# Decoder layer step on one core: the causal mask as a small matrix product, and the attention output stored in two halves

## The chip, the cores and the metric

The kernel runs on one core of a Trainium2 chip. A core has five engines with a queue of instructions each: PE (matrix products, with its weight loads listed as PEld), DVE (vector), ACT (scalar), POOL (GpSimd) and SP (which here issues most of the DMAs; POOL issues some). Each engine takes its queue in order and waits on semaphores of the others. PE writes its products into PSUM, in banks of 512 fp32 columns; DVE and ACT read PSUM, POOL does not. The metric is the device time of one execution in microseconds (us). Three runs of the kernel before gave 1462.22, 1463.86 and 1467.49 us, so the median is 1463.86 us.

## The reference, cut to what matters

```python
def fox_attend(q, k, v, cq, ck, q_pos):
    s = jnp.einsum('bqhd,bkhd->bhqk', q, k).astype(jnp.float32) * (HEAD_DIM ** -0.5)
    bias = jnp.transpose(cq, (0, 2, 1))[..., :, None] - jnp.transpose(ck, (0, 2, 1))[..., None, :]
    k_pos = jnp.arange(k.shape[1], dtype=jnp.int32)
    mask = k_pos[None, :] <= q_pos[:, None]
    s = jnp.where(mask, s + bias, NEG_INF)
    p = jax.nn.softmax(s, axis=-1).astype(v.dtype)
    return jnp.einsum('bhqk,bkhd->bqhd', p, v)
...
    q, k, v, logf, u = project_in(hp, w_in[i], b_f[i])
    att = fox_prompt(q, k, v, logf)                      # 8 heads, 1024 tokens, blocks of 128 rows
    ssm, sr, si = s5_mixer(u, h0, h0, *ssm_args)
    hp = post_mixer(hp, jnp.concatenate([att, ssm], axis=-1), p_prompt[i], *post_args)
...                                                      # the same for 32 sample tokens over a paged cache
    h1 = layer_norm(h + ..., ln1)                        # post_mixer: ALPHA*h + mix @ w_out, then the MLP
```

The model width is 1024: 512 columns of the mixer's output come from the attention over 8 heads of 64, and 512 from the state space part. Everything is fp32 to the outside.

## The kernel before, in words

fp32 precision is kept on PE by splitting an operand into a rounded part (type fp32r) and a rest: a product of two split operands is three products on PE (high by high, high by low, low by high). In the attention the scores are two products into one bank, of 68 and of 128 rows (line 872).

The program has these stages: layer norm and projections and the state space part (to about 310 us), the prompt's attention (about 310 to 516 us), the output projection with the second norm (to about 640 us), and the MLP (to the end). In the attention stage three streams are interleaved. `weights(h)` makes, for each of 8 blocks of 128 query rows, the scores of head h against all keys up to the diagonal: one bank when these are at most 512 keys, else two banks of equal width. The scores are held with the sign turned, so the softmax needs the row minimum `nm`, which is the bias of the exponential on ACT (line 882). A `tensor_reduce` on DVE takes the minimum over the first of two banks (line 876); over the last bank a `tensor_tensor_reduce` adds the mask tile `msk`, writes the masked scores back into the bank and takes the minimum at once (line 878; in the profile a CUSTOM_DVE instruction and a READ_ACCUMULATOR after it). The mask is 0 or +1e30, in the last 128 of 512 columns only. `values(h)` transposes the exponentials on PE (`tw`, line 900), copies them to SBUF on ACT (`pe`, line 904), rounds them on DVE (`ph`, line 905), takes the rest on POOL (`pl`), and multiplies both with the values, whose high and low parts lie side by side as 128 columns (lines 909, 910). So rows 0 to 63 of the bank `po` hold the high part's product and rows 64 to 127 the low part's. At the end of a half of 512 queries, ACT copies the low rows to `ol`, DVE adds them to the high rows into `oh`, and SP stores `oh` to `mixd` in DRAM (lines 912 to 916). There are 16 such halves. The third stream (`glu()` and `sample(bp)`) is background work that `fill` takes from by a time budget: the gate of the state space part, and the attention of the sample tokens, whose cache pages `pg` (64 of 256 KB) SP loads and whose value products are line 1035.

The output projection (`half`, line 1196) works through tiles of 128 tokens. For a tile it needs the state space columns of `mixd` (`load_mx`, line 1173), the attention columns (`load_at`, line 1213), which DVE multiplies by the reciprocal row sums `rb`, the split of both, and the split rows of `w_out` (`rawo`, `woh`, `wol`, from line 1157). Rows 512 to 1023 of `w_out` are loaded to a pool `woa`; rows 0 to 511 reuse memory of the attention's pool, so they come after the last half of the last head has been stored.

The order on each engine is not the order of the source: the build schedules the instructions of all engines by a model of their times, and memory that a tile takes over from another tile is part of what it waits for. A change of tile sizes or of operations therefore moves instructions elsewhere too.

Of the kernel before, what the change touches and what calls it, by code (L numbers as in the profile page):

```python
# [8 lines left out]
F32 = mybir.dt.float32  # L9
F32R = mybir.dt.float32r  # L10
# [4 lines left out]
AX = mybir.AxisListType  # L15
# [4 lines left out]
T = 1024  # L20
# [8 lines left out]
AW = 512  # L29
# [8 lines left out]
NEG = -1e30  # L38
# [3 lines left out]
IDENT, TRI, TRT, IOTA, SEL, QM, NM, BLK, OS, I16, OM, END = np.cumsum(  # L42
    [0, 128, 128, 128, 128, 256, 4, 4, 64, 16, 16, 512]).tolist()
# [26 lines left out]
def fox_s5_step(tc, a, o):  # L70
    nc = tc.nc
    V, S, G, PE, SY = nc.vector, nc.scalar, nc.gpsimd, nc.tensor, nc.sync
# [8 lines left out]
    def tt(e, out, x, y, op):  # L81
        e.tensor_tensor(out, x, y, op=op)  # L82
# [13 lines left out]
    MUL, ADD, SUB, MAX, MIN = ALU.mult, ALU.add, ALU.subtract, ALU.max, ALU.min  # L96

    cp = pool("const")
    dp = pool("dram", space=DRAM)
# [18 lines left out]
    cst = cp.tile([128, OM], F32, name="cst")  # L118
    ident = cst[:, IDENT:IDENT + 128]
# [3 lines left out]
    kkd = dp.tile([2, AW, NT], F32, name="kkd")  # L123
    vd = dp.tile([NT, AW], F32, name="vd")
    mixd = dp.tile([D, NT], F32, name="mixd")
    ud = dp.tile([4, 128, L * CB], F32, name="ud")
    yd = dp.tile([4, 128, L * CB], F32, name="yd")
    kd = dp.tile([NG, GH, 128], F32, name="kd")
# [81 lines left out]
    with ExitStack() as st0:  # L210
# [39 lines left out]
        for i, (t0, r) in enumerate(tiles):  # L250
# [3 lines left out]
            ps = bank2("pst").rearrange("p a (k c) -> p (a k) c", c=128)  # L254
# [11 lines left out]
            for k in range(KD):  # L266
                for j, (x, w) in enumerate(((hhi, wvh), (hhi, wvl), (hlo, wvh))):
                    if thin and j == 1:
                        PE.matmul(pv[:r], lhsT=x[:, k, t0:t0 + r], rhs=w[:, k], start=False, stop=(k == KD - 1),
                                  skip_group_check=True)  # L270
                    elif thin:
                        if j == 0:
                            PE.matmul(pv[:2 * r], lhsT=xx[:, k], rhs=w[:, k], start=(k == 0), stop=(k == KD - 1),
                                      skip_group_check=True)
                    else:
                        PE.matmul(pv[:r], lhsT=x[:, k, t0:t0 + r], rhs=w[:, k],
                                  start=(k == 0 and j == 0), stop=(k == KD - 1 and j == 2))
# [25 lines left out]
    with ExitStack() as st1:  # L303
# [20 lines left out]
        ps = flip()  # L324
# [114 lines left out]
        for dst, nm in ((crr, "c_re"), (cii, "c_im")):  # L439
# [3 lines left out]
            ps = flip()  # L443
# [6 lines left out]
        for dst, order in ((h0, ("state_re", "state_im")), (h0w, ("state_im", "state_re"))):  # L450
            t = ep.tile([128, 2, 2, HD], F32, tag="e", name="h0t")
            for j, nm in enumerate(order):
                SY.dma_start(out=t[:, :, j, :], in_=a[nm][0].rearrange("(u b) g p -> (b g) u p", u=2))
            ps = flip()
# [142 lines left out]
        def mixer(m):  # L597
# [65 lines left out]
            else:  # L663
# [7 lines left out]
                             in_=a["cache_logf"][0].rearrange("n t h -> n (t h)"),  # L671
# [27 lines left out]
        for c in range(3):  # L699
            ps = bank("mmf", "b")[0:40, :CH]  # L700
            for k in range(KD):
                for i, x in enumerate((hhi, hlo)):
                    PE.matmul(ps, lhsT=wf[:, k], rhs=x[:, k, c * CH:(c + 1) * CH],
                              start=(k == 0 and i == 0), stop=(k == KD - 1 and i == 1))
# [3 lines left out]
        ps = flip()  # L708
        for i, (t0, r) in enumerate(tiles):
# [16 lines left out]
                     in_=A[:, 0:64].rearrange("p (i h) -> p i h", h=8))  # L726
        SY.dma_start(out=a["o_fs"], in_=A[0:NS, 64:72])
        lf = ep.tile([8, NT], F32, tag="e", name="lf")
        for u in range(3):
            ps = flip()  # L730
            n = 4 if u < 2 else 1
            w_ = 0
            for i in range(n):
                t0, r = tiles[4 * u + i]
# [94 lines left out]
    aq_ = pool("attq", 2, stack=qctx, side="right")  # L829
# [2 lines left out]
    def slot(j, d=F32R):  # L832
        return (h1x, h1b)[j // 2].tile([128, 2 * L * CB], d, tag=f"u{j}", name="u", bufs=1)

    msk = aq_.tile([128, 512], F32, name="msk", bufs=1)
    G.memset(msk[:, 0:384], 0.0)
    G.tensor_copy(msk[:, 384:512], cst[:, TRI:TRI + 128])
    ins_, vs_, rows = {}, {}, {}

    def loads(h):  # L840
# [18 lines left out]
    def weights(h):  # L859
        qa, qb, ka, kb = ins_.pop(h)  # L860
        nm = ap_.tile([128, 8], F32, tag="nm", name="nm")
        for i in range(8):
            W = 128 * (i + 1)
            nb, n = (1, W) if W <= 512 else (2, W // 2)
            qs_ = slice(i * 128, i * 128 + 128)
            ss = []
            if nb == 2:
                nm1 = ap_.tile([128, 1], F32, tag="nm1", name="nm1")
            for c in range(nb):
                ps = bank("ss", "s")[:, 0:n]  # L870
                for x, y, kk in ((qb, kb, 68), (qa, ka, 128)):
                    PE.matmul(ps, lhsT=x[0:kk, qs_], rhs=y[0:kk, c * n:(c + 1) * n],
                              start=(kk == 68), stop=(kk == 128))
                ss.append(ps)
                if c < nb - 1:
                    V.tensor_reduce(out=nm1, in_=ps, axis=AX.X, op=MIN)
                else:
                    V.tensor_tensor_reduce(out=ps, in0=ps, in1=msk[:, 512 - n:512], scale=1.0,  # L878
                                           scalar=nm1 if c else -3.0 * NEG, op0=ADD, op1=MIN, accum_out=nm[:, i:i + 1])
            pr_ = ap_.tile([128, 512 * nb], F32, tag=f"row{nb}", name="row", bufs=4)  # L880
            for c, ps in enumerate(ss):
                S.activation(out=pr_[:, c * n:(c + 1) * n], in_=ps, func=AF.Exp, scale=-1.0, bias=nm[:, i:i + 1],  # L882
                             accum_out=lsum[:, h, i + 4 * c:i + 4 * c + 1])
            rows[h, i] = pr_
            yield

    def values(h):
        hs_ = slice(h * 64, h * 64 + 64)
        vr = vs_.pop(h)
        vv = ap_.tile([128, 8, 2, HD], F32R, tag="vv", name="vv")  # L890
        V.tensor_copy(vv[:, :, 0], vr)
        tt(G, vv[:, :, 1], vr, f(vv[:, :, 0]), SUB)
        for u in range(2):
            po = bank("po", "o")
            for j in range(4 * u + 4):
                i0 = max(j, 4 * u)
                n = 512 * (u + 1) - 128 * i0
                t = bank("tw", "t")[:, 0:n]
                for i in range(i0, 4 * u + 4):
                    PE.transpose(t[:, (i - i0) * 128:(i - i0) * 128 + 128], rows[h, i][:, j * 128:j * 128 + 128], ident)  # L900
                ph = ap_.tile([128, 512], F32R, tag="ph", name="ph", bufs=3)[:, 0:n]
                pl = ap_.tile([128, 512], F32R, tag="pl", name="pl", bufs=3)[:, 0:n]
                pe = ap_.tile([128, 512], F32, tag="pe", name="pe", bufs=4)[:, 0:n]
                S.copy(pe, t)
                V.tensor_copy(ph, pe)  # L905
                tt(G, pl, pe, f(ph), SUB)
                o = po[:, 512 - n:512]
                v = vv[:, j].rearrange("p a d -> p (a d)")
                PE.matmul(o, lhsT=v, rhs=ph, start=(j == 0), stop=False, skip_group_check=True)
                PE.matmul(o, lhsT=v, rhs=pl, start=False, stop=(j == 4 * u + 3), skip_group_check=True)  # L910
                yield
            ol = ap_.tile([64, 512], F32, tag="ol", name="ol", bufs=1)
            S.copy(ol, po[64:128])
            oh = ap_.tile([64, 512], F32, tag="oh", name="oh", bufs=2)
            tt(V, oh, po[0:64], ol, ADD)
            SY.dma_start(out=mixd[hs_, u * 512:u * 512 + 512], in_=oh)


    bg, bgt = [], [0.0, 0.0]
# [206 lines left out]
    ap_ = pool("att", 2, stack=actx)  # L1126
# [37 lines left out]
    for k in range(4, 8):  # L1164
        load_wo(k, woa, wp, V)
    mixv = mixd.rearrange("(k p) t -> p k t", p=128)
    dv = "p (c n) -> p c n"
    mxs, pss, order = {}, {}, [0, 1, 2, 3, 4, 5, 8, 6, 7]

# [40 lines left out]
    def load_at(i):  # L1210
        t0, r = tiles[i]
        mx = mxs[i][0]
        SY.dma_start(out=mx[:, 0:4, :r], in_=mixv[:, 0:4, t0:t0 + r])
        if t0 < T:
            rb = rbs.pop(i)
            tt(V, mx[:, 0:4, :r], mx[:, 0:4, :r], rb[:, :, :r], MUL)

# [3 lines left out]
    t = bank("trl", "t")[0:64, 0:128]  # L1221
# [12 lines left out]
    op = pool("out", 2, stack=smctx)  # L1234
# [47 lines left out]
    for n, i in enumerate(order):  # L1282
        t0, r = tiles[i]
# [20 lines left out]
        nb, rs = ln_norm(op, [z[:r, :512], z[:r, 512:]], r)  # L1304
# [20 lines left out]
    with ExitStack() as st1:  # L1325
# [24 lines left out]
        for m in range(8):  # L1350
# [21 lines left out]
            if m < 4:  # L1372
                k = m
# [369 lines left out]
```

## Time and profile before

| | |
|---|---|
| profiled execution | 1465.46 us |
| its span, first to last instruction | 1463.7 us |
| mean granted clock of PE | 0.979 of 2.4 GHz |
| PE busy | 1385.4 us (95%) |
| DVE busy | 993.2 us (68%) |
| ACT busy | 634.2 us (43%) |
| POOL busy | 675.1 us (46%) |

Busy time of PE is that of pipelined products, whose ends are modelled, so a product of 512 columns counts 0.4 us where the next one starts 0.23 us later. What a product costs in a dense stretch is read from the distance between the starts of neighbours, and lost time from the rows that name a wait. Idle time in brackets is that of the engine just before the instruction, with what ended it.

### The profile page before, as it was taken

Reading aid. Unit: us, or ns where it says so; the run is one execution under the profiler, and the core shown is the slowest. Engines: PE = TensorE matmul, PEld = TensorE weight load, DVE = VectorE, ACT = ScalarE, POOL = GpSimd, SP = SyncE. Lnnn points to the kernel's source line nnn. Section 1 sums busy time; section 2 is a strip of 40 time slices with the busy share of each in tenths; the row PEclk is TensorE's granted clock in tenths of the full one; section 3 lists DMA queues with packets and bytes.
Section 4 is the critical chain, followed back from the end, with each engine's and each line's share of the span. In section 5 each row is a group of like instructions: output and inputs, shape, how many; then the busy total and the mean of one; then the engine's idle time right before and its main releaser. Section 6 shows DMA issues by size and latency. Waiting matters only on the chain. (4 is left out here: it accounts for less than half of the span.)

```text
span 1463.7 us, 26623 instructions
## 1 busy us (share of the span) xinstructions
PE 1385.4 (95%) x10045; PEld 1269.7 (87%) x10045; DVE 993.2 (68%) x1591; ACT 634.2 (43%) x1188; POOL 675.1 (46%) x627
## 2 busy tenths in 40 slices
PE   6997999979999899999999999999999999999796
PEld 4787898977767657799999999999999999999786
DVE  8559599658867745568836545455455887878877
ACT  4423434446766624443324544444455344443212
POOL 4313012026665500037745443344337777777835
PEclk8999999999999999999999999999999999999998
DMA  7574355596776573222234344433376334444212
GB/s 278 174 139 103 97 146 140 165 245 174 180 190 156 150 245 91 80 74 87 79 99 154 133 147 162 162 124 134 134 277 212 119 126 153 162 162 133 74 32 101
DMA packets 205736, 211.89 MB, mean 145 GB/s; under 512 B 43592, under 2 KB 166088, under 8 KB 205608
## 3 DMA queue, kind: packets, MB, share of 16 engines
q1 hardware_dynamic: 197288, 178.02, 42.0%
q0 software_dynamic: 8320, 32.18, 5.7%
q8 instruction: 79, 1.29, 0.4%
q14 instruction: 49, 0.40, 0.1%
HBM read 143.59 MB, written 66.55 MB: 144 GB/s over the span
## 5 line engine op out<-in xcount | busy, mean ns | idle before, releaser
L1408 PE MATMUL pd<-x,a 128*128 128x264 f32 x1344 | 173.7, 289 | 14.2 <-DVE pacc L82 10.1
L1408 PEld LDWEIGHTS pd<-x,a 128*128 128x128 f32 x1344 | 169.5, 192 | 15.7 <-issue 10.0
L157 ACT CAST a<-s 128x256 fp32r<-128x256 f32 (+1 forms) x176 | 82.2, 483 | 200.5 <-POOL s L82 75.8
L82 DVE TENSOR_TENSOR pacc<-pd,pacc 128x528 f32<-128x528 f32 x180 | 121.4, 700 | 58.3 <-PE pd L1408 54.2
L82 DVE TENSOR_TENSOR wlo<-raw,whi 128x1024 fp32r<-128x1024 f32 x68 | 103.4, 1521 | 48.3 <-ACT whi L157 36.5
L1408 PE MATMUL pb<-th,a 128*128 128x264 f32 x768 | 132.3, 284 | 0.0
L82 POOL TENSOR_TENSOR pl<-pe,ph 128x512 fp32r<-128x512 f32 (+1 forms) x96 | 100.3, 1054 | 66.5 <-DVE ph L905 40.6
L82 POOL TENSOR_TENSOR a<-s,a 128x256 fp32r<-128x256 f32 x112 | 99.3, 892 | 60.4 <-ACT a L157 60.2
L82 POOL TENSOR_TENSOR s<-raw 128x256 f32<-128x256 f32 (+1 forms) x72 | 72.1, 1006 | 87.6 <-DVE a L82 64.0
L1408 PEld LDWEIGHTS pb<-th,a 128*128 128x128 f32 x768 | 109.2, 189 | 0.0
L1408 PE MATMUL pd<-x,whi 128*128 128x264 f32 x672 | 109.1, 284 | 0.0
L82 DVE TENSOR_TENSOR x<-x 128x1056 fp32r<-128x1056 f32 (+2 forms) x67 | 94.4, 1439 | 2.5 <-ACT x L1429 1.9
L183 PE MATMUL mmc<-hhi,whi 128*128 128x352 f32 x288 | 94.5, 328 | 0.0
L183 PE MATMUL mmc<-hhi,wlo 128*128 128x352 f32 x288 | 94.3, 327 | 0.0
L82 POOL TENSOR_TENSOR rs<-rs,mh 128x1 f32<-128x1 f32 (+1 forms) x27 | 20.5, 769 | 159.6 <-DVE rs L86 157.3
L1408 PEld LDWEIGHTS pd<-x,whi 128*128 128x128 f32 x672 | 93.7, 189 | 0.0
L183 PE MATMUL mmc<-hlo,whi 128*128 128x352 f32 x288 | 93.6, 325 | 0.0
L82 DVE TENSOR_TENSOR a<-s,a 128x512 fp32r<-128x512 f32 x64 | 48.0, 755 | 47.4 <-ACT a L157 43.2
L1408 PE MATMUL pb<-tl,a 128*128 128x264 f32 x384 | 78.1, 285 | 0.0
L157 ACT CAST whi<-raw 128x1024 fp32r<-128x1024 f32 x48 | 50.4, 1050 | 57.3 <-PE pa L1408 27.1
L882 ACT ACTIVATE row<-ss,nm 128x384 f32<-128x384 f32 (+4 forms) x96 | 55.5, 583 | 38.9 <-DVE nm L878 37.5
L1408 PE MATMUL pd<-x,wlo 128*128 128x264 f32 x336 | 68.2, 285 | 0.0
(471 smaller groups left out, 3959.9 us busy)
## 6 DMA issues: line engine op xcount, KB each, us to landing
x<-gd SPq DMA_DIRECT2D x53, 528.0 KB
raw<-in_w_up_dram SPq DMA_DIRECT2D x32, 512.0 KB
raw<-in_w_down_dram SPq DMA_DIRECT2D x128, 128.0 KB
gd<-e POOLq DMA_DIRECT2D x14, 1056.0 KB, 7.3
gd<-c POOLq DMA_DIRECT2D x14, 792.0 KB, 5.3
pg<-in_cache_k_dram SPq DMA_DIRECT2D x32, 256.0 KB
pg<-in_cache_v_dram SPq DMA_DIRECT2D x32, 256.0 KB
raw<-in_w_in_dram SPq DMA_DIRECT2D x12, 512.0 KB
```

The costliest lines, as they stand in the source:

```text
L82: e.tensor_tensor(out, x, y, op=op)
L157: S.copy(hi, x)
L183: PE.matmul(out, lhsT=wt[:, k], rhs=xt[:, k, c0:c0 + n], start=(k == 0 and i == 0), stop=(k == nk - 1 and i == 2))
L882: S.activation(out=pr_[:, c * n:(c + 1) * n], in_=ps, func=AF.Exp, scale=-1.0, bias=nm[:, i:i + 1], accum_out=lsum[:, h, i + 4 * c:i + 4 * ...
L1408: PE.matmul(ps[:, p, :PC], lhsT=wt[:, k], rhs=xt[:, k, p * PC:(p + 1) * PC], start=(start and k == 0 and j == 0), stop=(k == n - 1 and j = ...
```

## The change

Three things change in the source. The mask becomes a product on PE: an fp32r identity `idr_` as weights and a 128 by 128 fp32r mask tile `msk`, added into the last 128 columns of the last bank of each block; the row minimum is then a plain `tensor_reduce` per bank, and where there are two banks a `tensor_tensor` on 128 by 1 elements takes the smaller. The end of a half copies all 128 rows of `po` at once on ACT; SP stores the upper rows to `mixd` and the lower ones to a new DRAM tile `mixl`. The sum of the two is made in the projection: after the load of a tile's attention columns, POOL issues a DMA from `mixl` that adds into the loaded tile.

```diff
+    mixl = dp.tile([AW, T], F32, name="mixl")
...
-    msk = aq_.tile([128, 512], F32, name="msk", bufs=1)
-    G.memset(msk[:, 0:384], 0.0)
-    G.tensor_copy(msk[:, 384:512], cst[:, TRI:TRI + 128])
+    msk, idr_ = (aq_.tile([128, 128], F32R, name=n, bufs=1) for n in ("msk", "idr_"))
+    G.tensor_copy(msk, cst[:, TRI:TRI + 128])
+    G.tensor_copy(idr_, ident)
...
             if nb == 2:
-                nm1 = ap_.tile([128, 1], F32, tag="nm1", name="nm1")
+                nm1 = ap_.tile([128, 2], F32, tag="nm1", name="nm1")
             for c in range(nb):
                 ps = bank("ss", "s")[:, 0:n]
                 for x, y, kk in ((qb, kb, 68), (qa, ka, 128)):
                     PE.matmul(ps, lhsT=x[0:kk, qs_], rhs=y[0:kk, c * n:(c + 1) * n],
-                              start=(kk == 68), stop=(kk == 128))
+                              start=(kk == 68), stop=(kk == 128 and c < nb - 1), skip_group_check=True)
+                if c == nb - 1:
+                    PE.matmul(ps[:, n - 128:n], lhsT=idr_, rhs=msk, start=False, stop=True, skip_group_check=True)
                 ss.append(ps)
-                if c < nb - 1:
-                    V.tensor_reduce(out=nm1, in_=ps, axis=AX.X, op=MIN)
-                else:
-                    V.tensor_tensor_reduce(out=ps, in0=ps, in1=msk[:, 512 - n:512], scale=1.0,
-                                           scalar=nm1 if c else -3.0 * NEG, op0=ADD, op1=MIN, accum_out=nm[:, i:i + 1])
+                V.tensor_reduce(out=nm1[:, c:c + 1] if nb == 2 else nm[:, i:i + 1], in_=ps, axis=AX.X, op=MIN)
+            if nb == 2:
+                tt(V, nm[:, i:i + 1], nm1[:, 0:1], nm1[:, 1:2], MIN)
...
-            ol = ap_.tile([64, 512], F32, tag="ol", name="ol", bufs=1)
-            S.copy(ol, po[64:128])
-            oh = ap_.tile([64, 512], F32, tag="oh", name="oh", bufs=2)
-            tt(V, oh, po[0:64], ol, ADD)
-            SY.dma_start(out=mixd[hs_, u * 512:u * 512 + 512], in_=oh)
+            oh = ap_.tile([128, 512], F32, tag="oh", name="oh", bufs=2)
+            S.copy(oh, po)
+            SY.dma_start(out=mixd[hs_, u * 512:u * 512 + 512], in_=oh[0:64])
+            SY.dma_start(out=mixl[hs_, u * 512:u * 512 + 512], in_=oh[64:128])
...
+    mixlv = mixl.rearrange("(k p) t -> p k t", p=128)
...
         SY.dma_start(out=mx[:, 0:4, :r], in_=mixv[:, 0:4, t0:t0 + r])
         if t0 < T:
+            G.dma_start(out=mx[:, 0:4], in_=mixlv[:, :, t0:t0 + r], accum_op=ADD)
             rb = rbs.pop(i)
```

PE's queue at the start of head 0, blocks 0 to 2 (`ss` the score banks), before:

```order
L872 MATMUL ss<-kb,qb 128x128
L872 MATMUL ss<-ka,qa 128x128
L872 MATMUL ss<-kb,qb 128x256
L872 MATMUL ss<-ka,qa 128x256
L872 MATMUL ss<-kb,qb 128x384
L872 MATMUL ss<-ka,qa 128x384
```

The same place after the change, whose lines are numbered one higher from the new DRAM tile on:

```order
L873 MATMUL ss<-kb,qb 128x128
L873 MATMUL ss<-ka,qa 128x128
L876 MATMUL ss<-msk,idr__3106 128x128
L873 MATMUL ss<-kb,qb 128x256
L873 MATMUL ss<-ka,qa 128x256
L876 MATMUL ss<-msk,idr__3106 128x128
L873 MATMUL ss<-kb,qb 128x384
L873 MATMUL ss<-ka,qa 128x384
L876 MATMUL ss<-msk,idr__3106 128x128
```

One product of 128 columns is added behind the scores of each block, 64 in all.

POOL's queue at the end of the attention, with the last head's two halves of `pl` and the projection's norms (`rs`), before:

```order
L82 TENSOR_TENSOR pl<-pe,ph 128x512
L82 TENSOR_TENSOR pl<-pe,ph 128x384
L82 TENSOR_TENSOR pl<-pe,ph 128x256
L82 TENSOR_TENSOR pl<-pe,ph 128x128
L82 TENSOR_TENSOR pl<-pe,ph 128x512 x5
L82 TENSOR_TENSOR pl<-pe,ph 128x384
L82 TENSOR_TENSOR pl<-pe,ph 128x256
L82 TENSOR_TENSOR pl<-pe,ph 128x128
L82 TENSOR_TENSOR rs<-rs,mh 128x1 x6
```

The same place after the change (`mx<-mixl` are the adding loads):

```order
L82 TENSOR_TENSOR pl<-pe,ph 128x128
L1216 DMA mx<-mixl 128x4x128 x2
L82 TENSOR_TENSOR pl<-pe,ph 128x512 x5
L82 TENSOR_TENSOR pl<-pe,ph 128x384
L82 TENSOR_TENSOR pl<-pe,ph 128x256
L82 TENSOR_TENSOR pl<-pe,ph 128x128
L1216 DMA mx<-mixl 128x4x128 x2
L82 TENSOR_TENSOR rs<-rs,mh 128x1
L1216 DMA mx<-mixl 128x4x128
L82 TENSOR_TENSOR rs<-rs,mh 128x1
```

Two adding loads, of the projection's tiles 0 and 1, now stand in front of the `pl` of the last head's second half, and the other six stand among the norms.

PE's queue in the projection of the first tiles, where the last value products of the sample tokens (`po<-pg`) stand, before:

```order
L1035 MATMUL po<-pg,u 32x512 x2
L1196 MATMUL pso<-woh_6017,whi 128x512 x4
L1035 MATMUL po<-pg,u 32x512 x2
L1196 MATMUL pso<-wol_6018,whi 128x512
L1196 MATMUL pso<-woh_6017,wlo 128x512
L1196 MATMUL pso<-wol_6018,whi 128x512
L1196 MATMUL pso<-woh_6017,wlo 128x512
```

After the change they stand behind the last products with the state space rows of `w_out`, ahead of the first with the attention rows (`woh_6000`):

```order
L1197 MATMUL pso<-wol_5766,whi 128x512
L1197 MATMUL pso<-woh_5765,wlo 128x512
L1035 MATMUL po<-pg,u 32x512 x4
L1035 MATMUL po<-u,pnT 32x512 x4
L1045 MATMUL tpo<-cst,om 128x16 x4
L1197 MATMUL pso<-woh_6000,whi 128x512 x4
```

The scheduler has moved the second half of the sample attention ahead, so that its last products stand before the projection's attention rows instead of among and behind them. Four casts of `w_out` rows 512 to 1023, which stood at the end of the attention on ACT and DVE, stand early in the attention after the change.

## Rows read from the trace of the kernel before

**Rows 1.** Stretch table, attention: length, busy us (PE, PEld, DVE, ACT, POOL), clock, DMA.

```profile
310.00:520.00 210.00, 198.49 (x1336) 151.85 (x1336) 156.61 (x340) 129.11 (x345) 116.11 (x113) 0.96 0.70 175
```

**Rows 2.** Waits of PE's weight loads, 310 to 620 us: us in total, times, longest.

```profile
PEld po L1035 <- DMA pg<-in_cache_v_dram: 4.8, 3, 2.2
PEld po L910 <- POOL pl L82: 4.1, 6, 2.0
PEld pso L1196 <- ACT whi L1183: 3.9, 2, 3.1
PEld ss L872 <- ACT row L882: 3.7, 10, 0.8
...
PEld tw L900 <- ACT pe L904: 2.1, 4, 1.3
...
PEld po L909 <- DVE oh L82: 1.1, 1, 1.1
```

**Rows 3.** Timeline of PE around three products of 128 columns: start, us.

```profile
515.87 0.22 PE L910 MATMUL po<-pl,vv 128*128 128x128 f32 x1
515.93 0.45 PE L1196 MATMUL pso<-woh,whi 128*128 128x512 f32 x1
...
559.61 0.60 PE L1266 MATMUL psh<-cst,z 128*128 128x128 f32 x4
```

**Rows 4.** Groups of DVE in the attention stage: count, busy us, mean ns, idle before.

```profile
L878 DVE CUSTOM_DVE_ANT_0 ss<-ss,msk,nm 128x320 f32<-128x320 f32 (+3 forms) x32 | 20.9, 652 | 6.8 <-PE ss L872 5.5 <-ACT sg L1103 0.5 <-ACT pe L904 0.2
...
L876 DVE TENSOR_REDUCE nm<-ss 128x1 f32<-128x320 f32 (+3 forms) x32 | 18.6, 582 | 3.4 <-PE ss L872 3.4
...
L878 DVE CUSTOM_DVE_ANT_0 ss<-ss,msk 128x128 f32<-128x128 f32 (+3 forms) x32 | 15.8, 498 | 18.3 <-PE ss L872 11.7 <-PE po L910 4.3 <-ACT sg L1103 1.5
...
L82 DVE TENSOR_TENSOR oh<-po,ol 64x512 f32<-64x512 f32 x16 | 10.8, 676 | 3.5 <-ACT ol L913 3.5
...
L878 DVE DVE_READ_ACCUMULATOR2_ANT nm<- 128x1 f32 x64 | 8.8, 137 | 0.0
```

**Rows 5.** Timeline of DVE: an operation on 128 by 1 elements.

```profile
551.37 0.16 DVE L91 SCALAR_TENSOR_TENSOR nb<-mv,rs 128x1 f32<-128x1 f32 x1 [0.37 <-POOL rs L82]
```

**Rows 6.** Groups of ACT by shape, attention stage: copies from PSUM.

```profile
L904 ACT COPY pe<-tw 128x512 f32<-128x512 f32 x48 | 26.9, 592 | 7.5 <-PE tw L900 6.3 <-POOL pl L82 1.1
...
L913 ACT COPY ol<-po 64x512 f32<-64x512 f32 x16 | 9.3, 583 | 4.6 <-PE po L910 4.3
```

**Rows 7.** Timeline of PE in the projection, 530 to 542 us.

```profile
530.46 1.09 PE L1196 MATMUL pso<-woh,whi 128*128 128x512 f32 x4
...
535.20 1.04 PE L1035 MATMUL po<-pg,u 128*32 128x512 f32 x2 [1.79 <-DMA pg<-in_cache_v_dram]
537.12 1.73 PE L1035 MATMUL po<-pg,u 128*32 128x512 f32 x2 [0.87 <-DMA pg<-in_cache_v_dram]
538.77 2.07 PE L1196 MATMUL pso<-woh,whi 128*128 128x512 f32 x4
540.77 1.05 PE L1035 MATMUL po<-pg,u 128*32 128x512 f32 x4
```

**Rows 8.** Timeline of ACT at the end of the attention.

```profile
516.13 0.58 ACT L913 COPY ol<-po 64x512 f32<-64x512 f32 x1 [2.66 <-PE po L910]
...
521.89 1.05 ACT L157 CAST woh<-rawo 128x1024 fp32r<-128x1024 f32 x1 [1.03 <-DMA rawo<-in_w_out_dram]
```

**Rows 9.** Timeline of SP's DMAs at the end of the attention: start, us to issue.

```profile
517.46 0.49 SPq L916 DMA_DIRECT2D mixd<-oh  x1
518.04 1.50 SPq L1160 DMA_DIRECT2D rawo<-in_w_out_dram  x3
```

**Rows 10.** Operations of POOL, ns min/median/max: the subtraction `pl`, and a DMA it issues.

```profile
L82 POOL TENSOR_TENSOR pl<-pe,ph x96: 447/1164/3095, 328.6 to 509.4; 128x512 fp32r<-128x512 f32 x48, 128x384 fp32r<-128x384 f32 x16, 128x256 fp32r<-128x256 f32 x16, 128x128 fp32r<-128x128 f32 x16
...
L1515 POOL DMA_DIRECT2D gd<-e x14: 781/781/788, 784.6 to 1046.6; - x14
```

**Rows 11.** DMA issues of POOL in the program: size, us from issue to landing.

```profile
accd<-sgp POOLq DMA_DIRECT2D x8, 528.0 KB, 3.0
```

## Prediction

> **What bounds the kernel now.** I read the stretch table first, to see which engine is full where the change acts. In the attention PE is busy 198.49 of 210 us, DVE 156.61, ACT 129.11, POOL 116.11, at 0.96 of the upper clock level, 2.4 GHz [rows 1]. So an instruction added on PE costs its own time, and one taken from another engine gives only what PE waited for it. That is read from the second view, the waits of PE's weight loads [rows 2]: pages of the cache 4.8 us, `pl` 4.1, the state space split `whi` 3.9, `row` 3.7, `pe` 2.1, `oh` 1.1. These waits, not the 56 us of DVE work that disappears, are all that the change can win. The timelines of PE and ACT then show how the attention hands over to the projection.
>
> The profiled execution took 1465.46 us; the sum is made against it. It lies 1.6 above the median of the runs, 1463.86, to which I apply the result.
>
> **1. The mask on PE.** 8 heads by 8 blocks are 64 products of 128 columns. A single one starts 0.06 us before its successor, 515.87 to 515.93 [rows 3]; four that follow each other take 0.60 us where one takes 0.22, so (0.60 − 0.22) / 3 = 0.13 us each with nothing between [rows 3]. The products of masks stand between wide ones, like the first row, but their weights must be loaded too. I take 0.085, nearer the single one: 64 × 0.085 = **+5.4 us**, with ends 64 × 0.06 = +3.8 and 64 × 0.13 = +8.3. All of it is on PE and nothing covers it but the waits of step 2.
>
> The Trainium skill, page "TensorE: Matmul & The Clock Gate", section "Back-to-back issue gap", puts the spacing in a stream of weight load and product pairs at about 81 ns for 128 columns. As an estimate of that page the term would be 64 × 0.081 = 5.2 us; the trace's two rows lie on either side of it.
>
> **2. DVE.** Gone are the two forms of the fused minimum, 20.9 + 15.8 us, their 64 register reads, 8.8, and 16 sums `oh`, 10.8: 56.3 us [rows 4]. New are 32 reductions on the second of two banks, of the shape of the present first ones, 32 × 0.582 = 18.6 [rows 4]; 32 on a single bank, for which I take the fused one less the difference seen between the forms, 0.498 − (0.652 − 0.582) = 0.428, so 13.7; and 32 minima on 128 by 1 at 0.16, 5.1 [rows 4, 5]. That makes 37.4, net −18.9 of 156.6 us. DVE isn't the bound, so the 18.9 counts only through PE's waits for the chain from scores over `row` and `pe` to `pl`: 3.7 + 2.1 + 4.1 + 1.1 = 11.0 us [rows 2]. The first product after the scores sees its minimum earlier by 0.137 + 0.07 us less 0.16, next to nothing for two banks, and by 0.2 for one; the bank of `po` no longer waits for ACT and then DVE (0.583 + 0.676), but for one copy of 0.592 [rows 4, 6]. What is late next are the pairs of `pl` on POOL, which the change leaves alone. I take about half, **−5 us**, between 0 and −11.
>
> ACT copies 128 rows where it copied 64: 592 against 583 ns [rows 6], nothing. SP issues 16 more stores of 0.49 us [rows 9], 7.8 us of a queue that has 210; hidden, while the pages do not stand behind a store that waits for ACT.
>
> **3. The sample attention moved ahead.** Today its last value products stand among the projection's first. There PE waits for pages (4.8 us in three waits [rows 2], two of them seen as idle time of PE, 1.79 and 0.87 [rows 7]), and after the waits a run of products goes at about half speed: 2.07 for four `pso` where 1.09 is normal and 1.73 for two page products where 1.04 is, 1.7 us in all [rows 7]. In the new order most page products stand in the last head, and the last four behind all products with the state space rows. So 4.8 + 1.7 = 6.5 can go; against that the pages must now land earlier, while the attention already uses the DMA engines at 0.70 of their time [rows 1], and a page that is late there is a wait of the same kind. I take **−6 us**, between 0 and −6.5.
>
> **4. The state space columns.** PE waits 3.9 us, once for 3.1, for `whi` [rows 2], the split of the first tiles. In the new order these products begin in the last half but one, and the four casts of `w_out` which stood on ACT at the end are early. I take **−3 us**, between 0 and −3.9. It is not more because ACT, freed there, takes the copies of 128 rows next.
>
> **5. The end of the attention.** The last half is copied (0.58 [rows 8]), stored twice (2 × 0.49 [rows 9]), and only then may the rows 0 to 511 of `w_out` and the tiles 4 to 7 be loaded. From the issue of `rawo` at 518.04 to its cast at 521.89 are 3.85 us [rows 8, 9], and the cast takes 1.05. That is 0.58 + 0.98 + 3.85 + 1.05 = 6.5 us. PE has behind its last `po` 12 products at (1.09 − 0.45) / 3 = 0.21 us [rows 3, 7] and eight page and closing products, together some 4.5 us; so 2 us are uncovered, where today pages filled them. The subtraction for `wol` may add one more.
>
> The added wait is on POOL: two adding loads stand ahead of the last eight `pl`, and behind them waits PE's `po`. POOL is held from the copy of the half before: 0.58, stores 0.98, their landing 3.0 (as an estimate that of a DMA to DRAM that POOL issues [rows 11]), SP's load 0.49 and landing 3.0, two issues at 0.78 [rows 10], and the first `pl`, 1.16: 10.8 us. PE has in that time 25 projection products (5.3), 25 transposes (at 0.11 to 0.13, about 3), six page products (some 3): 11.3. It is just covered. The other six loads stand among single-column norms and delay nothing that is urgent. Together **+3 us**, between 0 and +8, where +8 is an uncovered 6.5 and 1.5 of the hold.
>
> Sum: 5.4 − 5 − 6 − 3 + 3 = −5.6, so 1459.9 for the profiled execution and **1458 us** for the median. Best ends: 3.8 − 11 − 6.5 − 3.9 = −17.6; worst: 8.3 + 8 = +16.3.
>
> **The rivals.**
> *The masks eat the gain (about 1464).* PE's waits may only change their name: DVE freed of 12% gives −2 instead of −5, and the pages moved into the attention wait there for half of the 6.5. Then 5.4 − 2 − 3 − 3 + 3 = +0.4. For it speaks that PE has 198.49 busy of 210 us [rows 1]; against it that `whi` and two page waits are single gaps at one place which the new order leaves.
>
> *POOL's adding loads decide (about 1472, slower).* POOL's `pl` takes 1164 ns in the median but up to 3095 [rows 10]: something holds POOL. If an issue is stretched the same way, from 0.78 to 3.1, the two in front of `pl` add 4.6 to a hold of 10.8 and PE waits 4.1; of the six others the four of the second half come when nothing is loaded ahead and add 4 × 2.3 = 9.3 behind the attention. −5.6 + 4.1 + 9.3 = +7.8. It decides from the point where the hold passes the 11.3 us of cover. Against it: the 14 issues of `gd` lie between 781 and 788 ns [rows 10], none stretched, though in a stretch where DVE does other work.
>
> The Trainium skill, page "SBUF — State Buffer", section "SBUF: two separate sides", says that a DMA issued by GpSimd is starved of its descriptors while DVE holds the port that the two share. By that rule this rival would hold, and the attention, where DVE is busy three quarters of the time, is the place. The issue rows at hand don't show it, the spread of `pl` agrees.
>
> *More goes than I count (about 1449).* If the chain had slack only where DVE was late, all 11.0 go: 5.4 − 11 − 6.5 − 3.9 + 1 = −15. For it: the waits for `row`, ten of them, are short, below 0.8 us [rows 2], the size of one DVE instruction. Against it: the longest for `pl` is 2.0 and belongs to POOL.
>
> *The change doesn't act as written:* the scheduler's new order could wait for something that the order doesn't show. I count it with the first rival.
>
> **How the numbers follow.** About 0.5%, 7.3 us, is what a measurement of this kernel can tell from no change. Forecast 0.47 (own range 1453 to 1463; 0.20 of it faster by over 0.5%, 0.26 within, 0.01 slower), masks eat the gain 0.18 (0.01, 0.15, 0.02), POOL's loads 0.17 (0.02 within, 0.15 slower), more goes 0.18 (all faster). Sums: faster 0.39, within 0.43, slower 0.18. The range reaches from beyond the third rival, 1447, to near the second, 1470.
>
> **What would show it.** Step 1: 64 products of 128 columns, whose successors start 0.06 to 0.13 us after them. Step 2: DVE busy near 138 us in the attention, and less in the waits for `row`, `pe` and `pl`. Step 3: no wait for pages among the projection's products; if the waits for pages in the last two heads rise by as much, it failed. Step 4: no wait for `whi` over 1 us. Step 5: between the last `po` and the first product with the attention's rows of `w_out` a gap of 2 to 3 us, and no wait of PE for POOL at the last half's first `pl`; the adding loads' issue at 0.78 us. The forecast is wrong if PE waits there for several us, or if the attention stage as a whole gets longer than 210 us.

## The result and the profile after: slower by 20 us

The changed kernel takes 1486.16 us in the median of 4 runs (1484.23 to 1491.36), the kernel before 1465.67 in the same comparison. The ratio is 1.0137 with a 95% interval of 1.0111 to 1.0163, so +20 us over before, where 1458 was forecast, and beyond the upper end of the range, 1470. The profiled execution has a span of 1489.6 us against 1463.7, that is +25.9.

The place is quickly found. The products of the projection with all 128 rows begin later and end later. Each line gives count, duration in ns (least, median, most), first and last start in us, and the form; first the changed kernel, then the kernel before:

```profile
L1197 PE MATMUL pso<-woh,whi x128: 391/396/796, 515.7 to 653.7; 128*128 128x512 f32 x128
```

```profile
L1196 PE MATMUL pso<-woh,whi x128: 389/396/792, 507.8 to 630.1; 128*128 128x512 f32 x128
```

23.6 of the 25.9 us are lost by there. The stretch tables of the changed kernel, the first stretch to be held against [rows 1]:

```profile
310.00:520.00 210.00, 196.26 (x1323) 152.61 (x1324) 140.62 (x280) 120.55 (x332) 110.41 (x105) 0.95 0.67 171
```

```profile
520.00:660.00 140.00, 130.46 (x609) 96.09 (x608) 71.42 (x145) 52.36 (x103) 25.49 (x25) 0.95 0.55 140
```

and the second stretch of the kernel before:

```profile
520.00:660.00 140.00, 136.23 (x713) 104.49 (x712) 76.45 (x156) 57.44 (x113) 17.75 (x18) 0.99 0.40 119
```

DVE fell from 156.61 to 140.62 us, near the 138 foreseen, but PE, ACT and POOL did less as well: in the same 210 us less of the work got done. PE's clock fell from 0.99 to 0.95 behind 520. The waits of PE's weight loads, 310 to 620 us (total, times, longest), against [rows 2]:

```profile
PEld po L911 <- POOL pl L82: 7.4, 12, 1.3
PEld po L1035 <- DMA pg<-in_cache_v_dram: 6.7, 2, 5.4
...
PEld ss L873 <- ACT row L883: 5.3, 8, 1.8
...
PEld ssm L973 <- DVE u L86: 4.1, 1, 4.1
...
PEld pso L1197 <- ACT whi L1184: 0.7, 1, 0.7
```

The waits for `pl`, for pages and for `row` all grew (4.1, 4.8 and 3.7 before), where the forecast let them shrink; a single wait for the first vector of the sample tokens (`u`) takes 4.1 us, where 0.7 was. The wait for `whi` shrank, from 3.9 to 0.7. What DVE does for the minima, as groups of its instructions from 310 to 556 us (busy us, mean ns):

```profile
L878 DVE TENSOR_REDUCE nm<-ss 128x1 f32<-128x384 f32 (+4 forms) x96 | 51.9, 552 | 29.8 <-PE ss L876 23.3 <-PE ss L873 5.5
L82 DVE TENSOR_TENSOR nm<-nm 128x1 f32<-128x1 f32 x32 | 12.4, 387 | 0.2
```

The reductions cost 51.9 us, as foreseen (18.6 kept, 18.6 and 13.7 new, together 50.9). But the 32 minima on 128 by 1 elements take 387 ns each and not the 160 of [rows 5]. One of them, with what stands around it, from the timeline of all engines (start, us):

```profile
409.74 0.63 DVE L878 TENSOR_REDUCE nm<-ss 128x1 f32<-128x448 f32 x1
...
410.53 0.97 DVE L906 CAST ph<-pe 128x384 fp32r<-128x384 f32 x1 [0.17 <-PE ss L873]
...
411.43 0.68 DVE L878 TENSOR_REDUCE nm<-ss 128x1 f32<-128x512 f32 x1
411.65 0.99 POOL L82 TENSOR_TENSOR pl<-pe,ph 128x384 fp32r<-128x384 f32 x1 [0.36 <-DVE ph L906]
...
412.03 0.63 DVE L82 TENSOR_TENSOR nm<-nm 128x1 f32<-128x1 f32 x1
...
412.69 0.63 ACT L883 ACTIVATE row<-ss,nm 128x448 f32<-128x448 f32 x1 [0.64 <-DVE nm L82]
```

Two things are to be seen. The second bank's minimum is there at 410.37, but the instruction that combines both stands behind a cast and behind the next block's reduction, and starts at 412.03. And then it ends with POOL's `pl`, at 412.66. The exponential, which frees the score banks, waited 2.3 us for an operation of 0.15. Of the 32 minima in this trace 15 begin while POOL is idle (one of them 0.02 us before the end of a `pl`) and take 150 ns on average. The other 17 begin beside a running operation of POOL, end within 0.03 us of the end of that or the next one, and take 595.

The Trainium skill, page "SBUF — State Buffer", section "SBUF: two separate sides", says that a DVE operation with two inputs in SBUF and a GpSimd operation that reads SBUF share a port pair as an exclusive lock, and that whichever starts second is blocked for the whole of the other. The rows agree: 0.15 us alone, and to the end of `pl` beside it.

### The profile page after: what moved, and what is told of

The parts are those of the page before. It is cut to its first block, busy times and chain, and to the rows that moved or that the text cites. A ratio compares the mean times of both kernels' runs of the same rounds, so it can differ in the third digit from the quotient of the medians.

```text
span 1489.6 us, 26703 instructions
## 1 busy us (share of the span) xinstructions
PE 1400.1 (94%) x10109; PEld 1283.0 (86%) x10109; DVE 986.2 (66%) x1543; ACT 632.5 (42%) x1188; POOL 689.2 (46%) x635
## 5 line engine op out<-in xcount | busy, mean ns | idle before, releaser
L82 POOL TENSOR_TENSOR pl<-pe,ph 128x512 fp32r<-128x512 f32 (+1 forms) x96 | 103.5, 1087 | 82.8 <-DVE ph L906 63.8
L82 POOL TENSOR_TENSOR s<-raw 128x256 f32<-128x256 f32 (+1 forms) x72 | 75.4, 1051 | 85.2 <-DVE a L82 63.8
L906 DVE CAST ph<-pe 128x512 fp32r<-128x512 f32 (+1 forms) x96 | 52.4, 561 | 31.7 <-ACT pe L905 20.1
```

## Experiments

Theories at the start: Q, the waits in SP's queue and for pages; M, the 64 products; H, the halves with POOL's adding loads. From the second group of kernels on: L, the minimum's wait for POOL; O, chance of the scheduler's order; C, the separate minimum lets other work in between. Differences in us are the ratio times 1466.

**mask_only.** The mask part of the change with the old end of a half.

```diff
-            S.copy(oh, po)
...
+            S.copy(ol, po[64:128])
...
+            tt(V, oh, po[0:64], ol, ADD)
...
-            G.dma_start(out=mx[:, 0:4], in_=mixlv[:, :, t0:t0 + r], accum_op=ADD)
```

> Only the mask product and the plain minimum; the halves are summed on DVE and stored once, as before. Theory Q (queues and waits: of the +20 us the 64 products are about 5, the rest is waiting that the new order makes, at SP's stores and pages): +5 to +12 us over before. Theory M (the 64 products on a full PE are most of the loss): +15 to +20. Theory H (two stores per half and POOL's adding loads are most of it): +5 or less.

1486.14 us, ratio 1.0137 (1.0102 to 1.0172): the whole loss, +20. H falls, Q's range is passed, and M's upper end is met.

**halves_only.** The other part alone: `S.copy(oh, po)`, two stores and the adding load, with the mask as before.

> Only the copy of both halves, the two stores and the adding loads; the mask as before on DVE. Q: +5 to +12 us over before, with waits of PE for pages or for what stands behind a store on SP. M: 0 or a gain of some us. H: +13 or more, with PE waiting for the pl behind POOL's adding loads.

1470.68 us, ratio 1.0026 (1.0009 to 1.0042): +4, with an interval of 1.3 to 6.2, so at the low end of what Q wanted or under it, and far from H's +13.

**no_mask_product.** The changed kernel without the products.

```diff
-                if c == nb - 1:
-                    PE.matmul(ps[:, n - 128:n], lhsT=idr_, rhs=msk, start=False, stop=True, skip_group_check=True)
```

> The changed kernel without the 64 mask products, so the scores are not masked; the reductions and all else stay. Q: 5 us less than the changed kernel (about 1481), give or take what a shifted order does. M: 15 us less or more (1471 or below). H: 5 less.

1490.47 us, ratio 1.0163 (1.0129 to 1.0197). The scores are then not masked, so it serves for timing alone. It is no faster without the products (the interval overlaps that of the changed kernel), where all three theories wanted less time: M falls. What is left for the loss is what DVE got, or the order.

**act_stores.** Both stores of a half on ACT: `S.dma_start` for `SY.dma_start`.

> The changed kernel with both stores of a half issued by ACT, which made the copy, instead of SP, so that SP's loads of heads and pages no longer stand behind a store that waits for ACT. Q: 5 to 10 us less than the changed kernel (1476 to 1481), and the 3.7 us wait for the sample's first vector near 353 us gone. M and H: no change beyond 0.3%, or a little slower for 32 more issues on ACT.

1489.44 us, ratio 1.016 (1.0126 to 1.0194). Against Q: taking the stores out of SP's queue gained nothing. The wait for the sample's first vector was gone, but PE stood 3.4 us before the same product, now for `row`.

**one_bank_only** and **two_bank_only.** Mask product and plain minima only in blocks with one bank, or only in blocks with two. Only the latter have the 128 by 1 minimum.

```diff
+                if nb == 1:                                 # in two_bank_only: if c == 1
+                    PE.matmul(ps[:, n - 128:n], lhsT=idr_, rhs=mskr, start=False, stop=True, skip_group_check=True)
```

> The kernel before with the mask product and plain minimum only in the 32 blocks of one bank; blocks of two banks stay as before, so no 128x1 minimum exists. L: 0 to +4 us over before (32 products, 2.5 us). O: +8 or more is possible, as another order.

> The kernel before with the mask product, plain minima and 128x1 minimum only in the 32 blocks of two banks. L: most of the loss, +14 to +20 us over before. O: not more than the kernel with the one-bank blocks changed.

1466.68 us, ratio 1.0001 (0.9988 to 1.0013), and 1484.49 us, ratio 1.0122 (1.0095 to 1.0149). The loss lies in the two-bank blocks, as L wanted.

**before_plus_min** and **before_plus_reduce.** The kernel before with 32 more instructions that change no value, once with two operands, once with one (there the fused minimum writes to the second column of `nm1`, which is two columns wide):

```diff
+            if nb == 2:
+                tt(V, nm[:, i:i + 1], nm[:, i:i + 1], nm1, MIN)                       # before_plus_min
+                V.tensor_reduce(out=nm[:, i:i + 1], in_=nm1, axis=AX.X, op=MIN)       # before_plus_reduce
```

> The kernel before with one more 128x1 minimum of nm and nm1 behind each masked reduction over two banks (32 in all, the value does not change). L: +8 us or more over before. O: another order by chance, so anything from 0 to +10, not tied to the durations of these 32.

> The kernel before with 32 more reductions over a 128x2 tile at the places of the 32 extra minima of the run before (before_plus_min, +21 us). Every engine has the same instructions in the same order as there; only the kind of these 32 differs (one operand in SBUF instead of two). Theory L (the wait of the two-operand form for POOL makes the loss): +0 to +5 us over before. Theory O (the order makes it): +16 or more, as there.

1487.91 us, ratio 1.0139 (1.012 to 1.0157), and 1482.62 us, ratio 1.009 (1.007 to 1.011). The first run shows the loss without any product or any change of the reductions over the scores. In the two traces the instructions stand in the same order on every engine, and the two intervals do not meet, so their 7 us are the two operands' alone. The groups of DVE, first with two operands, then with one:

```profile
L82 DVE TENSOR_TENSOR nm<-nm,nm 128x1 f32<-128x1 f32 x32 | 12.2, 381 | 0.2
```

```profile
L882 DVE TENSOR_REDUCE nm<-nm 128x1 f32<-128x2 f32 x32 | 4.7, 146 | 0.2
```

12.2 − 4.7 = 7.5 us of DVE in the chain came back as 7 us of the kernel. But 13 stay, with instructions of 0.15 us: above L's range and below O's, so L is only a third. What the other two thirds can be shows before_plus_min's timeline:

```profile
342.02 0.74 DVE L878 CUSTOM_DVE_ANT_0 ss<-ss,msk,nm 128x512 f32<-128x512 f32 x1
...
342.69 0.13 DVE L878 DVE_READ_ACCUMULATOR2_ANT nm<- 128x1 f32 x1
342.69 0.71 DVE L88 TENSOR_SCALAR sg<-sg 128x1088 f32<-128x1088 f32 x1
344.21 0.22 DVE L86 TENSOR_SCALAR u<-u 64x4 f32<-64x4 f32 x1 [0.81 <-DMA u<-pcd]
...
344.86 0.16 DVE L82 TENSOR_TENSOR nm<-nm,nm 128x1 f32<-128x1 f32 x1
...
345.55 0.58 PE L872 MATMUL ss<-kb,qb 68*128 68x256 f32 x1 [3.20 <-ACT row L884]
```

The fused minimum is complete at 342.82. The added instruction comes 2 us later, behind the gate `sg` and behind an operation that waits for a DMA, all three score banks are held meanwhile, and PE stands 3.20 us. (The bank that lets PE go on is that of the next, one-bank block, whose own fused minimum stood behind the same wait for a DMA.) From 310 to 660 us PE's score products wait for `row`, that is for an exponential that frees a bank, as these lines show (total, times, longest): in the kernel before, in before_plus_min and in before_plus_reduce.

```profile
PE ss L872 <- ACT row L882: 0.2, 1, 0.2
```

```profile
PE ss L872 <- ACT row L884: 8.3, 7, 3.2
```

```profile
PE ss L872 <- ACT row L885: 7.3, 5, 4.1
```

So in this pair PE does wait for score banks, which it hardly did before.

**min_by_reduce**, **mask_min_reduce**, **min_scalar.** The one-operand reduction in the changed kernel and in mask_only; and in the changed kernel `ts(V, nm, nm1[:, 0:1], nm1[:, 1:2], MIN)`, whose second operand is a scalar per row.

> The changed kernel with the smaller of the two minima taken by a reduction over the 128x2 tile (one operand in SBUF) instead of a product of two 128x1 operands. In the changed kernel's trace that small operation takes 0.15 us where POOL is idle and 0.57 where a subtraction pl runs on POOL (18 of 24 between 320 and 520 us start so). Theory L (DVE waits there for POOL, the exponential and PE's next scores behind it, and most of the +20 us come from that): 10 us or more below the changed kernel, 1476 or less, no such operation over 0.2 us. Theory O (the loss lies in the order that the scheduler now chooses, whatever the operations cost): within 6 us of the changed kernel.

> Mask products, plain minima and the minimum by a reduction over 128x2, but the halves summed on DVE and stored once as before. L: +5 to +9 over before (products 5, and 32 operations more in the chain), 4 below the changed kernel with the reduction, the price that the halves alone showed. O: as the mask alone, +20.

> The changed kernel with the minimum as an operation of one tensor operand and a per-row scalar operand, both in SBUF. If only a second tensor operand makes DVE wait for POOL: 0.15 to 0.2 us each also beside a pl, and about 1480. If the scalar operand does so too: up to 1.2 us beside a pl, and about 1486.

1479.57 us, ratio 1.0093 (1.0072 to 1.0113); 1480.97 us, 1.0089 (1.0071 to 1.0107); 1487.49 us, 1.0141 (1.0119 to 1.0164). The first two gain 6.5 and 7 us, about as in the pair of equal order, and lie between what L and what O wanted. (The minima beside POOL in the changed kernel's trace are 17 of 32, counted as above, not 18 of 24.) min_scalar is a miss for L: its 32 instructions take 192 to 215 ns whatever POOL does, and it gained nothing.

**reduce_no_product.** min_by_reduce without the 64 products.

> The changed kernel with the minimum by a reduction over 128x2, and without the 64 mask products (the scores are not masked). L: 4 to 7 us below the same kernel with the products (1479.6), so 1473 to 1476. O: a new order, between 1470 and 1490, and no relation to 64 x 0.08.

1488.81 us, ratio 1.014 (1.0109 to 1.0172): again not faster, and 7 us slower than with them, though the two intervals overlap a little. L misses. It is not explained; its order differs, so a difference of order may be worth that much here.

**after_fused_zero** and **mask_fused_zero.** The separate minimum goes: for the second bank one instruction adds zeros and takes both minima.

```diff
-            if nb == 2:
-                tt(V, nm[:, i:i + 1], nm1[:, 0:1], nm1[:, 1:2], MIN)
...
+                    V.tensor_tensor_reduce(out=ps, in0=ps, in1=zer[:, 0:n], scale=1.0, scalar=nm1[:, 0:1],
+                                           op0=ADD, op1=MIN, accum_out=nm[:, i:i + 1])
```

> The changed kernel, but in the 32 blocks of two banks the minimum of the second bank and the smaller of both come from one instruction, as before the change (it adds a tile of zeros instead of the mask, which PE has added). Theory C (a separate combining minimum lets other DVE work in between, the three score banks are held longer, PE waits): +3 to +8 us over before (halves 4, 64 products up to 5), and the exponential again 1.5 to 1.7 us after the last score. Theory O (chance of the order): +12 or more.

> The same without the change of the halves: mask products and plain minima, the combining minimum fused, halves summed on DVE. C: 0 to +5 over before, which is what the 64 products cost. O: +12 or more.

1477.12 us, ratio 1.0074 (1.0047 to 1.0101), and 1473.7 us, ratio 1.0036 (1.0022 to 1.0049). With the mask alone the loss falls from +20 to +5, with both parts from +20 to +11. The second lies at the upper end of C's range and far below O's. The first lies between the two ranges, with an interval (+7 to +15) that reaches into both; its exponential starts 1.65 us after the scores, as C wanted.

**min_reduce_adj2.** min_by_reduce with DVE's casts and reductions queued by hand before or behind the pair.

> The changed kernel with the minimum by a reduction over 128x2, and with the second bank's reduction queued behind the casts that were emitted before it and later casts and reductions behind the combining minimum, so that other work stands between the two in 7 of 32 blocks instead of 29. C: 3 to 8 us below the same kernel without that (1479.6), unless the forced order makes DVE wait elsewhere; the exponential 1.7 us or less after the last score. O: no relation.

1515.22 us, ratio 1.0308 (1.0268 to 1.0348): +45. In the trace the second reduction now starts 2.7 us after its scores on average instead of 0.4, since it waits behind casts: the delay was moved in front of the pair. It doesn't tell what the pair alone would give.

The kernels in one table, without the two that leave the products out and the one ordered by hand. "Exponential" is the time from the end of PE's last product of a two-bank block's scores (the mask's included) to the start of its first exponential on ACT, the mean of 32 blocks; "held" the time from a bank's first score product to the end of its exponential, the mean of 96. Both are worked out from the single instructions of the traces.

| minimum of two banks | kernel | us over before | exponential, us | held, us |
|---|---|---|---|---|
| fused | before | 0 | 1.63 | 3.85 |
| fused | one_bank_only | 0 | 1.47 | 3.69 |
| fused | halves_only | 4 | 1.66 | 3.82 |
| fused | mask_fused_zero | 5 | 1.54 | 3.93 |
| fused | after_fused_zero | 11 | 1.65 | 3.90 |
| separate, one operand | before_plus_reduce | 13 | 2.55 | 4.74 |
| separate, one operand | mask_min_reduce | 13 | 2.26 | 4.60 |
| separate, one operand | min_by_reduce | 14 | 2.37 | 4.65 |
| separate, two operands | two_bank_only | 18 | 2.64 | 4.69 |
| separate, two operands | mask_only | 20 | 2.46 | 4.76 |
| separate, two operands | the changed kernel | 20 | 2.37 | 4.66 |
| separate, two operands | before_plus_min | 20 | 2.70 | 4.86 |
| separate, two operands | act_stores | 23 | 2.22 | 4.46 |
| separate, row scalar | min_scalar | 21 | 2.31 | 4.43 |

No separate minimum comes out under 13, no fused one over 11; the intervals of those two neighbours overlap (+10 to +16 and +7 to +15). The fused kernels and the separate ones differ in both times as well. But among the separate ones these times do not order the loss: mask_min_reduce and min_scalar start the exponential after 2.26 and 2.31 us and lose 13 and 21.

## Why the prediction was wrong

The step that failed is the second: "32 minima on 128 by 1 at 0.16, 5.1", off the path, with "the first product after the scores sees its minimum earlier by 0.137 + 0.07 us less 0.16, next to nothing for two banks". I priced the new instruction by its duration from [rows 5] and took for granted that it follows its reduction. Measured, it starts on average 0.69 us after the second bank's minimum (here and in the next numbers the mean of the 32 blocks), takes 0.39, and the exponential starts 2.37 instead of 1.63 us after the scores. Before the change nothing could come in between, because one instruction did both and its accumulator was read right behind it [rows 4]. With three score banks, each held 0.8 us longer, PE's next scores wait. This step was to give −5 us; its separate minimum cost 15 with the mask alone (20 − 5) and 9 with both parts (20 − 11), each give or take some 5.

No rival named it. The second rival had POOL in it, but by its DMA issues; the section that I cited there, "SBUF: two separate sides" of the Trainium skill's page "SBUF — State Buffer", has the rule on the port pair too, and I weighed only its sentence on descriptors. So even the worst end of the sum, +16.3, lay below the result.

The other steps:

- **Step 1 was right in size.** In the changed kernel's trace the successor of a mask product starts 0.06 us after it in the median, and 0.088 in the mean, without the three behind which PE waits for 0.3 us or more: 3.8 to 5.6 us for 64. mask_fused_zero puts the products, with the plain minima of the one-bank blocks, at +5.3 us (3.2 to 7.2), against +5.4. That this agrees to 0.1 is luck: in one_bank_only 32 products and the same plain minima cost 0.1 us (−1.8 to 1.9) and not half of 5.3.
- **Step 3 was wrong in sign.** The pages moved into the last head, and the wait grew from 4.8 to 6.7 us. There are six page buffers. The products on the old pages are through at 530.99, SP loads the buffers again from 532.12, behind four loads of `rb` that it issued from 528.45, and the first new page is used at 540.16. In the meantime PE runs out of other products; that the projection would have had more of them is my reading, and no run shows it. SP's DMAs there (start, us to issue):

```profile
532.12 5.11 SPq L938 DMA_DIRECT2D pg<-in_cache_v_dram  x6
```

And PE's timeline from there to the first attention rows of `w_out`, idle time in brackets:

```profile
540.16 1.92 PE L1035 MATMUL po<-pg,u 128*32 128x512 f32 x2 [5.04 <-DMA pg<-in_cache_v_dram]
...
550.79 0.50 PE L1197 MATMUL pso<-woh,whi 128*128 128x512 f32 x1 [0.68 <-ACT oh L914]
...
556.65 1.06 PE L1045 MATMUL tpo<-cst,om 128*128 128x16 f32 x8 [0.82 <-DVE om L82]
...
559.30 2.08 PE L1197 MATMUL pso<-woh,whi 128*128 128x512 f32 x4 [1.59 <-ACT woh L158]
```

- **Step 4 came true.** No wait for `whi` over 1 us is left: 0.7 where 3.9 was.
- **Step 5 was about right.** The idle time of PE between the last `po` and the attention rows is 0.68 + 0.82 + 1.59 = 3.1 us, then four products at half rate (2.08 us where 1.09 is normal [rows 7]). The halves alone cost 3.8 us (1.3 to 6.2) where +3 was taken, though that run also holds whatever the halves give in step 2. The hold of POOL was worked out rightly as a whole: from the start of the copy of the first half, 521.10, to the end of the first `pl` behind the adding loads, 531.57, are 10.5 us against 10.8. (POOL's idle time of 13.69 is longer because it had been done since 513.85.) Its parts differ: the issue of an adding load took 1.29 to 1.86 us, not 0.78. PE waited 0.91 us there, for the second `pl`. From ACT's and POOL's timelines:

```profile
521.10 0.59 ACT L914 COPY oh<-po 128x512 f32<-128x512 f32 x1 [2.36 <-PE po L911]
...
527.54 2.73 POOL L1216 DMA_DIRECT2D mx<-mixl  x2 [13.69 <-DMA mx<-mixd]
529.24 2.33 POOL L82 TENSOR_TENSOR pl<-pe,ph 128x512 fp32r<-128x512 f32 x1
```

The decline of PE's clock behind 520 us goes with these idle times: it makes each wait dearer than its own length, which the sum counted only where it would vanish.

Where PE loses the time can be added up over one stretch, from its first score product to its last projection product of 128 rows. Idle is the time in which neither a product nor a weight load runs, in pieces of over 0.05 us; the clock is the mean granted one, as a share of 2.4 GHz. Both are worked out from the traces.

| kernel | stretch, us | PE idle, us | of it until `row`, us | clock |
|---|---|---|---|---|
| before | 318.9 | 12.1 | 0.2 | 0.973 |
| mask_fused_zero | 327.0 | 14.0 | 0.6 | 0.965 |
| after_fused_zero | 327.7 | 15.1 | 0.8 | 0.968 |
| min_by_reduce | 332.7 | 16.1 | 1.0 | 0.959 |
| before_plus_reduce | 334.6 | 18.7 | 7.8 | 0.954 |
| before_plus_min | 339.4 | 20.6 | 8.3 | 0.948 |
| min_scalar | 341.3 | 23.4 | 2.8 | 0.954 |
| the changed kernel | 342.6 | 21.1 | 4.8 | 0.950 |

The changed kernel's stretch is 23.7 us longer. Of these 9.0 are idle time. What the clock takes from a stretch is (1 − clock) × its length: (1 − 0.950) × 342.6 = 17.1 instead of (1 − 0.973) × 318.9 = 8.6, so 8.5 more. The 64 products take about 5. For the other rows the same sum, with the products only where there are any, comes within 3 us of what the stretch gained; for mask_min_reduce (not in the table) it explains only 9 of 15.4.

In the two kernels that only add the separate instruction, practically all of the added idle time is the wait for `row`: there the chain from the late minimum over the held banks to PE is seen whole. In the changed kernel it is 4.6 of the 9.0; the waits for pages (+2.4) and for the sample's first vector (+3.4) stand beside it, and that for `whi` fell by 2.4. In min_by_reduce it is 0.8 of 4.0.

What stays open: how the separate minimum costs min_by_reduce 14 us with so little waiting for `row`, and how much of the 13 us of the one-operand form is the order that the scheduler builds around the instruction (the sample attention moved ahead is part of it). That order changes with every edit but in the one pair. For min_scalar the table shows where its gain went, into idle time (23.4 us, of which 5.4 for `pe`), but not why. The two kernels without products have as much idle time as the changed one (22.2 and 20.9 us) and a lower clock, 0.942 and 0.935 over the stretch, which takes 20 and 22 us; why it is lower is open.

No kernel here beats the one before. The nearest is one_bank_only, at 1.0001.

## What to carry to other kernels

A fused reduction that is split in two can cost more than the second instruction's time, since whatever the scheduler puts between the two lengthens the chain; so look for a fused form before moving work to another engine. Price a new instruction in a chain by when it can start and by how long it takes beside the other engines' work, not by its duration next to idle ones. A pair of kernels with the same order that differ in one operand tells such a price cleanly; elsewhere an edit brings its own order along.

## What the runs showed of the hardware

A minimum of two 128 by 1 operands in SBUF takes 0.15 us alone and up to 1.26 beside POOL's subtraction. With one operand, or with a scalar per row as the second, it takes at most 0.17 and 0.22 us in the traces here, whatever POOL does. An adding load that POOL issues takes 1.29 to 1.86 us to issue and 5.0 us in the median to land, against 0.78 to issue and 3.0 to land for the plain ones of [rows 10, 11], which are other transfers (the one of 3.0 moves 528 KB, an adding load 256 KB):

```profile
L1216 POOL DMA_DIRECT2D mx<-mixl x8: 1287/1360/1861, 527.5 to 623.0; - x8
```
